# Hybrid DiT trunk step on one core: the norm of branch C's heads in thirds, its factors and the residual gate sent to all partitions through DRAM

## The chip, the cores and the metric

One core of one Trainium2 chip. The metric is the device time of one execution in microseconds (us); smaller is better. The engines are TensorE (PE in the rows; PEld its weight loads), VectorE (DVE), ScalarE (ACT), GpSimd (POOL) and SyncE (SP), which issues every DMA of this kernel.

## The reference

Two layers of a trunk with three branches over 1152 tokens (128 context and 1024 latent), model width 1024. All branches are fed by one projection of the normed stream. What matters here is the end of branch C (differential attention, four heads of width 128) and the end of the layer:

```python
def diff_attn(q, k, v, lam, subln, lam_init):
    ...
        s = jnp.einsum('bqhmd,bshmd->bhmqs', qblk, k).astype(jnp.float32) * SCALE
        p = jax.nn.softmax(s, axis=-1)
        pd = p[:, :, 0] - lam * p[:, :, 1]
        return jnp.einsum('bhqs,bshe->bqhe', pd.astype(v.dtype), v)
    ...
    o = rmsnorm(o, subln) * (1 - lam_init)
    return o.reshape(B, T, D_C)

def mixer_tail(x, gate, oa, g_a, ob, g_b, oc, g_c, merge, P):
    ...
         + m[:, :, 2] * ((oc * jax.nn.silu(g_c)) @ P['w_br_c']))
    return x + gate * (y @ P['w_out'])
```

So each head's output is divided, token by token, by the root of its mean square over 128 channels, scaled per channel, and multiplied by a SiLU gate; and the layer's output is scaled by a gate row per channel (one for context, one for latent tokens) before it is added to `x`.

## The kernel before

The 1152 tokens are 9 tiles of 128. Float32 products are made of three fast products of high and low parts (`mm3`, L162 to L165), so operands are split: a ScalarE copy writes the high part, a VectorE or GpSimd subtraction the low one. A head of branch C is worked off in five groups of at most two tiles. For each group: `q_conv` (L434 to L446) copies the queries twice side by side into `qdup` (one half by VectorE, L437, one by ScalarE), transposes them (L442) and splits them into `qhl`; `c_probs` makes the scores (L540, L541), evacuates them with their row maxima (L542), takes the exponential (L552) and subtracts the two maps; `c_pv` transposes the probabilities (L569), splits them into `PT` and multiplies by V into `ps_o`; its result goes into `u.o`, a tile of 128 channels by 1152 tokens (`O` in the rows).

When a head is complete, `c_finish` (L580) makes its norm. Tokens lie along the free axis there, channels on partitions. ScalarE squares `u.o`; nine matmuls with a column of ones (L585) give the sums with tokens on partitions; a reciprocal root by VectorE (`rsq`, some twenty small operations) gives the 9 columns of factors. To bring a factor per token to all 128 partitions, three times three products of a broadcast column with the identity matrix (L593) write 128 x 384 into PSUM, from which VectorE multiplies (`stt`, L112 in the rows), and GpSimd multiplies with the gate. The head then goes to DRAM (`osp`), from where the tail of the layer reads it.

`gate_rows` (L1035) makes the residual gate for a quarter of the output projection by the same means: 4 products of a broadcast column with the identity (L1040) and two ScalarE copies into `gr`, four quarters a layer. VectorE reads `gr` once for each of the nine token tiles of a quarter.

What sets the order: the program is written as a sequence in Python, and a list scheduler fixes the order of each engine's instructions when the kernel is built; at run time each engine takes its list in order and waits on semaphores. `fg` marks code as foreground (`HPO`, L26, an offset of priority). The projections of the next head, the gates and other work are a generator, `background` (L755), of which `step(n)` (L768) takes n pieces after each group, by the table `BGQ` (L50). `flush` (L736) is called within `fg` after the scores of a group: it runs the pending product with V (`pend`) of the group before, and, one group later, the norm of the finished head (`done`). So a head's norm runs as foreground in the second group of the next head; that of the fourth head runs beside the first groups of branch A.

Tiles come from rings: a tag has a fixed number of buffers (`RINGS`, L54), taken in the order of the program, and a new tile waits until the last use of the one it replaces. Ring `E` has two buffers, and `qdup` lives there; `gr` is in `cx`, with one buffer. PSUM has 4 buffers of tag `s`, 3 of `t` and 1 of `o`.

Of the kernel before, what the change touches and what calls it, by code (L numbers as in the profile page):

```python
# [18 lines left out]
DEPTH = 2  # L19
# [45 lines left out]
def hybrid_dit_kernel(ctx, tc, I, O):  # L65
# [8 lines left out]
    def ps(tag, *shape):  # L74
        return psp.tile([128] + list(shape), F32, tag=tag, name="ps_" + tag, bufs=PSB[tag])

    def tl(tag, *shape, bufs=1):
        return big.tile([128] + list(shape), F32, tag=tag, name=tag, bufs=bufs)

    def al(tag, name, *shape):  # L80

        return big.tile([128] + list(shape), F32, tag=tag, name=name, bufs=RINGS[tag])
# [13 lines left out]
    def dma(out, in_):  # L96
        nc.sync.dma_start(out=out, in_=in_)

    def acopy(out, in_, scale=1.0):
        A.activation(out=out, in_=in_, func=AF.Copy, scale=scale)  # L100

    def tt(e, out, a, b, op):
        e.tensor_tensor(out=out, in0=a, in1=b, op=op)  # L103
# [7 lines left out]
    def stt(out, a, s, b, op0, op1):  # L111
        V.scalar_tensor_tensor(out=out, in0=a, scalar=s, in1=b, op0=op0, op1=op1)  # L112
# [3 lines left out]


    xres = drp.tile([NT, 128, DM], F32, name="xres")
    osp = [drp.tile([4, 128, NTOK], F32, name=f"osp{b}") for b in range(3)]
    xsp, gsp = (drp.tile([4, 128, NTOK], F32, name=n) for n in ("xsp", "gsp"))  # L120

# [456 lines left out]
        acopy(u.o[:, tiles[0] * 128:tiles[0] * 128 + w], po)  # L578

    def c_finish(L, u, h):  # L580
        sq = al("T", "sq", 1152)
        A.activation(out=sq, in_=u.o, func=AF.Square)
        p = ps("t", 9)
        for i in range(9):
            T.matmul(out=p[:, i:i + 1], lhsT=sq[:, i * 128:(i + 1) * 128], rhs=one, start=True, stop=True)  # L585
        e2 = tl("e2", 9)
        stt(e2, u.l0, EPS, u.l0, ALU.mult, ALU.mult)
        y = rsqrt(p, 9, 1.0 / 128, e2)
        for c in range(3):
            pb = ps("t", 3, 128)  # L590
            for t in range(3):
                i = 3 * c + t
                T.matmul(out=pb[:, t, :], lhsT=y[:, i:i + 1].to_broadcast([128, 128]), rhs=ident, start=True, stop=True)  # L593
            oc = u.o[:, c * 384:(c + 1) * 384].rearrange("p (t n) -> p t n", t=3)
            stt(oc, oc, L.D.sub1, pb, ALU.mult, ALU.mult)
            tt(Pq, u.o[:, c * 384:(c + 1) * 384], u.o[:, c * 384:(c + 1) * 384],
               u.gate[:, c * 384:(c + 1) * 384], ALU.mult)
        dma(osp[2][h], u.o)

# [126 lines left out]
    def unit_phase(L):  # L728
# [1 line left out]
        l = L.l  # L730
        a_groups = [CQA, CKA, CVA]
        pend = None

        done = None

        def flush():  # L736
            nonlocal pend, done
            d, done = done, None
            if pend:
                pend()  # L740
                pend = None
            if d:
                d()

        def start(h):
            u = Unit()
# [21 lines left out]
        def step(n):  # L768
            for _ in range(n):
                next(bg, None)  # L770

        def fg(f, *args):
            with tc.high_priority(offset=HPO):
# [258 lines left out]
                tail_branch(L, 2, j, c, ohl, wbs[j], ms[j - 6][:, c, :])  # L1032
                y_split(L, j, c)

    def gate_rows(D, q4, dst):  # L1035

        for s in range(2):
            p = ps("t", 2, 128)
            for k in range(2):
                T.matmul(out=p[:, k, :], lhsT=D.modt[:, 16 + 2 * q4 + k, s:s + 1].to_broadcast([128, 128]),  # L1040
                         rhs=ident, start=True, stop=True)
            acopy(dst[:, s, :], p.rearrange("p k n -> p (k n)"), scale=0.5)

    def x_in(l, i):
        if l:
# [14 lines left out]
    def w_out_phase(L, Ln):  # L1060
        l = L.l
        wtag = ("P", "S", "S", "P")
        wq = [load_wo(L, 0, wtag[0])]
        gr = None
        for q4 in range(4):
            cs = slice(q4 * 256, (q4 + 1) * 256)
            if q4 < 3:
                wq.append(load_wo(L, q4 + 1, wtag[q4 + 1]))
            w = wq[q4]
            gr = al("cx", "gr", 2, 256)  # L1070
            gate_rows(L.D, q4, gr)
            if q4 == 1 and Ln is not None:
                load_unit_consts(Ln)
                Ln.wu = load_wu(Ln, c_groups(0))
# [197 lines left out]
```

## Time and profile before

| | |
|---|---|
| median of 3 runs | 2887.47 us (2887.15 to 2888.11) |
| the profiled execution | 2884.63 us, of which its span is 2882.8 us |
| mean granted clock of TensorE | 0.98 of full speed |
| PE, DVE, ACT, POOL busy | 2740.5, 1773.3, 1284.2, 924.8 us |
| PE share of the span | 95% |

Busy time is that of the instructions themselves; waiting for a semaphore is not in it. In the rows, a line is a line of the kernel before (a helper's line where a helper issues the instruction: L97 is every DMA, L100 ScalarE's copies, L103 a tensor-tensor operation, L107 a tensor-scalar one, L112 `stt`), and buffer numbers are left out of names. "idle before" is how long the engine had stood still just before an instruction, with what released it. The granted clock (`PEclk`) is the share of full speed that TensorE was given in a stretch. The durations below are all from the profiled execution.

### The profile page before, as it was taken

The page shows a single profiled execution, that of the slowest core. Times are in us where ns is not written, and L with a number is a line of the kernel's source. Part 1 is how long each engine was busy: PE and PEld are TensorE (multiplying, and loading weights), DVE is VectorE, ACT ScalarE, POOL GpSimd, SP SyncE. Part 2 cuts the span into 40 slices and gives each one's busy share as a digit, 9 for nine tenths or more (in the row PEclk, how much of TensorE's full clock was granted, in tenths as well). Part 3 has the DMA queues.
Part 4 walks back from the last instruction along what each step waited for, and adds up shares of the span by engine and source line. Part 5 has one row for each costly group of instructions (what it writes and reads, how often), then busy time and mean ns, then how long its engine had stood idle before and what let it go on. Part 6 is the DMA issues. An engine that isn't in the chain of part 4 may idle for free.

```text
span 2882.8 us, 44242 instructions
## 1 busy us (share of the span) xinstructions
PE 2740.5 (95%) x16745; PEld 2648.5 (92%) x16745; DVE 1773.3 (62%) x4412; ACT 1284.2 (45%) x2577; POOL 924.8 (32%) x756
## 2 busy tenths in 40 slices
PE   8999999999998989998999999999999989999999
PEld 4889999999997989998989899998999989899989
DVE  5887878776646583116958887787665455311162
ACT  4464555566654631212144555555666456212110
POOL 1334354531234341213104252445212344322130
PEclk9999999999999999998999999999999999999999
DMA  6011011112222252114631010110112121311122
GB/s 228 25 33 34 19 32 42 36 48 74 70 73 65 65 159 68 52 39 144 195 100 36 22 34 19 33 48 31 55 64 80 63 70 60 114 44 49 49 90 85
DMA packets 231698, 190.74 MB, mean 66 GB/s; under 512 B 21746, under 2 KB 217660, under 8 KB 231484
## 3 DMA queue, kind: packets, MB, share of 16 engines
q1 hardware_dynamic: 231484, 187.92, 20.7%
q8 instruction: 131, 2.15, 0.3%
q14 instruction: 83, 0.68, 0.1%
HBM read 153.52 MB, written 34.35 MB: 65 GB/s over the span
## 4 chain that ended last, share of the span: by engine, by line
PE 71%; DVE 15%; ACT 5%; issue 4%; DMA 3%; POOL 1%; SPq 1%; DVEq 0%; ACTq 0%; POOLq 0%
PE ps_s L163 18%; PE ps_s L164 18%; PE ps_s L165 18%; PE ps_o L711 2%; PE ps_t L702 2%; DVE P L542 2%; PE ps_s L540 2%; DVE macc L112 2%; PE ps_t L569 1%; PE ps_s L541 1%; DMA modw<-in_mod_w_dram 1%; DVE lr L860 1%; DVE lr L112 1%; PE ps_o L164 1%; PE ps_s L662 1%
## 5 line engine op out<-in xcount | busy, mean ns | idle before, releaser
L163 PE MATMUL ps_s<-h,wsh 128*128 128x384 f32 x1920 | 660.0, 344 | 8.6 <-ACT mg L971 5.9
L165 PE MATMUL ps_s<-h,wsl 128*128 128x384 f32 x1920 | 654.4, 341 | 0.9 <-POOL wsl L103 0.9
L164 PE MATMUL ps_s<-h,wsh 128*128 128x384 f32 x1920 | 654.9, 341 | 0.0
L163 PEld LDWEIGHTS ps_s<-h,wsh 128*128 128x128 f32 x1920 | 364.3, 190 | 13.5 <-ACT mg L971 7.1
L165 PEld LDWEIGHTS ps_s<-h,wsl 128*128 128x128 f32 x1920 | 363.1, 189 | 2.0 <-POOL wsl L103 1.6
L164 PEld LDWEIGHTS ps_s<-h,wsh 128*128 128x128 f32 x1920 | 364.1, 190 | 0.6
L103 POOL TENSOR_TENSOR wsl<-wsraw,wsh 128x1024 fp32r<-128x1024 f32 x80 | 198.7, 2483 | 395.3 <-ACT wsh L100 229.6
L163 PE MATMUL ps_s<-uwh,h 128*128 128x384 f32 x864 | 296.9, 346 | 5.8 <-ACT h L100 2.8
L164 PE MATMUL ps_s<-uwl,h 128*128 128x384 f32 x864 | 293.9, 341 | 0.1
L165 PE MATMUL ps_s<-uwh,h 128*128 128x384 f32 x864 | 292.1, 344 | 0.0
L112 DVE SCALAR_TENSOR_TENSOR ps_s<-mg,ps_s 128x384 f32<-128x384 f32 x96 | 52.6, 559 | 359.7 <-PE ps_s L165 359.6
L103 POOL TENSOR_TENSOR qkraw<-qkraw,tab 128x384 f32<-128x384 f32 (+2 forms) x92 | 132.7, 1453 | 335.2 <-DVE qkraw L103 212.5
L542 DVE TENSOR_SCALAR_CACHE_REDUCE P<-ps_s 128x384 f32<-128x384 f32 (+1 forms) x400 | 205.5, 539 | 39.9 <-PE ps_s L541 38.7
L163 PE MATMUL ps_s<-oh,wb 128*128 128x384 f32 x576 | 196.0, 351 | 35.3 <-DVE yr L112 10.5
L103 DVE TENSOR_TENSOR PT<-ps_t,PT 128x512 fp32r<-128x512 f32 (+2 forms) x304 | 187.7, 625 | 59.5 <-ACT PT L100 58.0
L100 ACT ACTIVATE PT<-ps_t 128x512 fp32r<-128x512 f32 (+2 forms) x304 | 160.0, 546 | 125.1 <-PE ps_o L165 67.9
L552 ACT ACTIVATE P<-P,csm 128x1152 f32<-128x1152 f32 (+1 forms) x144 | 165.8, 1154 | 101.8 <-DVE csm L107 101.8
L164 PE MATMUL ps_s<-ol,wb 128*128 128x384 f32 x576 | 194.7, 346 | 0.0
L165 PE MATMUL ps_s<-oh,wb 128*128 128x384 f32 x576 | 194.5, 346 | 0.0
L971 ACT ACTIVATE mg<-ps_s 128x384 f32<-128x384 f32 x144 | 69.6, 485 | 266.1 <-PE ps_s L165 169.6
L163 PE MATMUL ps_s<-woh,yh 128*128 128x256 f32 x576 | 167.4, 291 | 11.7 <-DVE xt L103 6.5
L163 PEld LDWEIGHTS ps_s<-uwh,h 128*128 128x128 f32 x864 | 164.6, 191 | 9.4 <-ACT h L100 3.5
(253 smaller groups left out, 6364.6 us busy)
## 6 DMA issues: line engine op xcount, KB each, us to landing
wsraw<-in_w_in_dram SPq DMA_DIRECT2D x80, 512.0 KB, 3.7
wuraw<-in_w_in_dram SPq DMA_DIRECT2D x72, 192.0 KB, 3.5
ol<-osp SPq DMA_DIRECT2D x24, 576.0 KB, 5.0
modw<-in_mod_w_dram SPq DMA_DIRECT2D x16, 512.0 KB, 5.8
woraw<-in_w_out_dram SPq DMA_DIRECT2D x16, 512.0 KB, 4.4
modw<-in_mod_w_dram SPq DMA_DIRECT2D x14, 576.0 KB, 5.5
modw<-in_mod_w_dram SPq DMA_DIRECT2D x19, 384.0 KB, 4.3
wuraw<-in_w_in_dram SPq DMA_DIRECT2D x36, 128.0 KB, 2.3
```

What stands on the lines that cost most here:

```text
L100: A.activation(out=out, in_=in_, func=AF.Copy, scale=scale)
L103: e.tensor_tensor(out=out, in0=a, in1=b, op=op)
L112: V.scalar_tensor_tensor(out=out, in0=a, scalar=s, in1=b, op0=op0, op1=op1)
L163: T.matmul(out=out, lhsT=r(lh), rhs=r(rh), start=first, stop=False)
L164: T.matmul(out=out, lhsT=r(lh), rhs=r(rl), start=False, stop=False)
L165: T.matmul(out=out, lhsT=r(ll), rhs=r(rh), start=False, stop=last)
L540: T.matmul(out=p, lhsT=qh, rhs=kk, start=True, stop=False)
L542: V.tensor_scalar(out=S[:, n * c:n * c + n], in0=p, scalar1=1.0, scalar2=NEG, op0=ALU.mult, op1=ALU.max, accum_out=mx[:, mp, c:c + 1])
L552: A.activation(out=Ss[mp][:, 0:n], in_=Ss[mp][:, 0:n], func=AF.Exp, scale=0.125, bias=nm[:, mp:mp + 1], accum_out=acc)
L702: T.transpose(p[:, b, 128 * j:128 * j + 128], Ps[2 * t + j][:, (b0 + b) * 128:(b0 + b + 1) * 128], ident)
L711: T.matmul(out=po[:, t, :, :], lhsT=r(vs[kb]), rhs=r(x[:, b, :]), start=kb + k == 0, stop=k == 1 and kb == len(vs) - 1)
L971: A.activation(out=m, in_=p, func=AF.Tanh, scale=0.5)
```

## The change

`c_finish` becomes a generator. The squares are made in thirds of 384 tokens (tiles `sq` in ring E instead of T), the sums of a third are copied to `csum` by VectorE, and after each third it yields. The fourth piece makes the factors, transposes them into 9 rows (one transpose, L597 of the changed kernel), copies them (`yrow`, ring E) and writes the rows to DRAM (`ybd`); then, for each third, a DMA reads the three rows back to all 128 partitions (`yb`, ring E), VectorE multiplies from there, and GpSimd as before. `flush` no longer runs the norm but makes the generator `fin`, and `step` takes one piece of it beside each piece of `bg`; what remains is run when the next head's norm begins. `gate_rows` transposes the 16 columns of the gate once per layer (two transposes), and writes 8 rows to DRAM (`gbd`); for each quarter two DMAs read the rows of `gr` to all partitions.

```diff
+    ybd = drp.tile([4 * DEPTH, NT, 128], F32, name="ybd")
+    gbd = drp.tile([DEPTH, 8, 2, 128], F32, name="gbd")
...
     def c_finish(L, u, h):
-        sq = al("T", "sq", 1152)
-        A.activation(out=sq, in_=u.o, func=AF.Square)
-        p = ps("t", 9)
-        for i in range(9):
-            T.matmul(out=p[:, i:i + 1], lhsT=sq[:, i * 128:(i + 1) * 128], rhs=one, start=True, stop=True)
+
+        sums = tl("csum", 9)
+        for c in range(3):
+            sq = al("E", "sq", 384)
+            A.activation(out=sq, in_=u.o[:, c * 384:(c + 1) * 384], func=AF.Square)
+            p = ps("t", 3)
+            for t in range(3):
+                T.matmul(out=p[:, t:t + 1], lhsT=sq[:, t * 128:(t + 1) * 128], rhs=one, start=True, stop=True)
+            V.tensor_copy(sums[:, 3 * c:3 * c + 3], p)
+            yield
         e2 = tl("e2", 9)
         stt(e2, u.l0, EPS, u.l0, ALU.mult, ALU.mult)
-        y = rsqrt(p, 9, 1.0 / 128, e2)
+        y = rsqrt(sums, 9, 1.0 / 128, e2)
+        p = ps("t", 128)
+        T.transpose(p[0:9, :], y, ident)
+        row = al("E", "yrow", 128)
+        acopy(row[0:9, :], p[0:9, :])
+        yd = ybd[4 * L.l + h]
+        dma(yd, row[0:9, :])
         for c in range(3):
-            pb = ps("t", 3, 128)
-            for t in range(3):
-                i = 3 * c + t
-                T.matmul(out=pb[:, t, :], lhsT=y[:, i:i + 1].to_broadcast([128, 128]), rhs=ident, start=True, stop=True)
-            oc = u.o[:, c * 384:(c + 1) * 384].rearrange("p (t n) -> p t n", t=3)
-            stt(oc, oc, L.D.sub1, pb, ALU.mult, ALU.mult)
-            tt(Pq, u.o[:, c * 384:(c + 1) * 384], u.o[:, c * 384:(c + 1) * 384],
-               u.gate[:, c * 384:(c + 1) * 384], ALU.mult)
+            oc = u.o[:, c * 384:(c + 1) * 384]
+            yb = al("E", "yb", 3, 128)
+            dma(yb, yd[None, 3 * c:3 * c + 3, :].to_broadcast([128, 3, 128]))
+            stt(oc, oc, L.D.sub1, yb.rearrange("p t n -> p (t n)"), ALU.mult, ALU.mult)
+            tt(Pq, oc, oc, u.gate[:, c * 384:(c + 1) * 384], ALU.mult)
         dma(osp[2][h], u.o)
+        yield
...
             if d:
-                d()
+                for _ in fin:
+                    pass
+                fin = d() or iter(())
...
         def step(n):
             for _ in range(n):
                 next(bg, None)
+                next(fin, None)
...
-    def gate_rows(D, q4, dst):
-
+    def gate_rows(D):
+
+        p = ps("t", 2, 128)
         for s in range(2):
-            p = ps("t", 2, 128)
-            for k in range(2):
-                T.matmul(out=p[:, k, :], lhsT=D.modt[:, 16 + 2 * q4 + k, s:s + 1].to_broadcast([128, 128]),
-                         rhs=ident, start=True, stop=True)
-            acopy(dst[:, s, :], p.rearrange("p k n -> p (k n)"), scale=0.5)
+            T.transpose(p[0:8, s, :], D.modt[:, 16:24, s], ident)
+        row = al("E", "grow", 2, 128)
+        acopy(row[0:8], p[0:8], scale=0.5)
+        dma(gbd[D.l], row[0:8])
...
-        gr = None
+        gate_rows(L.D)
         for q4 in range(4):
...
             gr = al("cx", "gr", 2, 256)
-            gate_rows(L.D, q4, gr)
+            for s in range(2):
+                dma(gr[:, s, :].rearrange("p (k n) -> p k n", k=2),
+                    gbd[l, 2 * q4:2 * q4 + 2, s, :][None].to_broadcast([128, 2, 128]))
```

Lines of the changed kernel are two higher up to `c_finish`: its L444 is L442 of before, its L571 is L569, its L542 is L540, its L439 is L437. The order of the instructions changes at three places around the norm of a head; all three are shown for the first head of layer 0, whose norm runs in the second head. In the names, `ps_s<-uwh,h` and `ps_s<-uwl,h` are matmuls of the projection of the next head, `qdup` and `qhl` a group's queries before and after the transposes, `P` and `PT` probabilities, `O` the finished head.

First place: TensorE, at the identity products and at the next query transposes behind them. Before, the products,

```order
L163 MATMUL ps_s_2453<-uwh_2032,h_290 128x384
L593 MATMUL ps_t_2374<-ident_63,rsq_2360 128x128 x3
L593 MATMUL ps_t_2380<-ident_63,rsq_2360 128x128 x3
L593 MATMUL ps_t_2386<-ident_63,rsq_2360 128x128 x3
L164 MATMUL ps_s_2453<-uwl_2033,h_290 128x384
L165 MATMUL ps_s_2453<-uwh_2032,h_291 128x384
```

then seven more matmuls of the projection, and then:

```order
L164 MATMUL ps_s_2453<-uwl_2041,h_296 128x384
L165 MATMUL ps_s_2453<-uwh_2040,h_297 128x384
L442 MATMUL ps_t_2517<-ident_63,qdup_2513 128x128 x4
L569 MATMUL ps_t_2559<-ident_63,P_2302 128x128
L569 MATMUL ps_t_2559<-ident_63,P_2394 128x128
L569 MATMUL ps_t_2559<-ident_63,P_2302 128x128
```

Now, at the transpose of the factors:

```order
L165 MATMUL ps_s_2722<-uwh_2042,h_298 128x384
L597 MATMUL ps_t_2704<-ident_63,rsq_2690 9x128
L166 MATMUL ps_s_2722<-uwl_2043,h_298 128x384
L167 MATMUL ps_s_2722<-uwh_2042,h_299 128x384
L444 MATMUL ps_t_2786<-ident_63,qdup_2782 128x128
L571 MATMUL ps_t_2828<-ident_63,P_2495 128x128
L571 MATMUL ps_t_2828<-ident_63,P_2596 128x128
L571 MATMUL ps_t_2828<-ident_63,P_2495 128x128
L444 MATMUL ps_t_2786<-ident_63,qdup_2782 128x128
L571 MATMUL ps_t_2828<-ident_63,P_2596 128x128
L444 MATMUL ps_t_2786<-ident_63,qdup_2782 128x128 x2
L571 MATMUL ps_t_2842<-ident_63,P_2495 128x128
```

The products are gone; one transpose stands in a run of the projection's matmuls, whose last two stand between it and the query transposes.

Second place: VectorE, at the products with the factors. Before:

```order
L112 SCALAR_TENSOR_TENSOR P_2394<-P_2407,csm_2393,P_2394 128x1152
L112 SCALAR_TENSOR_TENSOR O_1350<-O_1350,sub1_529,ps_t_2374 128x384
L112 SCALAR_TENSOR_TENSOR O_1350<-O_1350,sub1_529,ps_t_2380 128x384
L112 SCALAR_TENSOR_TENSOR O_1350<-O_1350,sub1_529,ps_t_2386 128x384
L437 COPY qdup_2980<-uq_952 128x4x64
L103 TENSOR_TENSOR qhl_2516<-ps_t_2517,qhl_2516 128x512
L393 TENSOR_REDUCE qkss_2481<-qktmp_2480 128x12
L542 TENSOR_SCALAR P_2525,csm_2524<-ps_s_2526 128x384
```

Now:

```order
L112 SCALAR_TENSOR_TENSOR O_1352<-O_1352,sub1_531,yb_2709 128x384
L103 TENSOR_TENSOR rsq_2756<-rsq_2756 128x12
L112 SCALAR_TENSOR_TENSOR O_1352<-O_1352,sub1_531,yb_2713 128x384
L103 TENSOR_TENSOR rsq_2756<-rsq_2756 128x12
L439 COPY qdup_2782<-uq_954 128x4x64
L112 SCALAR_TENSOR_TENSOR rsq_2756<-rsq_2756 128x12
```

and, five small operations of `rsqrt` later:

```order
L112 SCALAR_TENSOR_TENSOR O_1352<-O_1352,sub1_531,yb_2717 128x384
L112 SCALAR_TENSOR_TENSOR rsq_2756<-rsq_2756 128x12
L439 COPY qdup_2991<-uq_954 128x4x64
L103 TENSOR_TENSOR qkraw_2748<-qkraw_2748,rsq_2756 128x768
L103 TENSOR_TENSOR PT_2833<-ps_t_2828,PT_2833 128x512
L103 TENSOR_TENSOR qhl_2785<-ps_t_2786,qhl_2785 128x512
```

The three products, which stood together, are spread between operations of another `rsqrt` (`rsq_2756`, of the projection's queries and keys); the `qdup` that L444 above reads now stands behind the second of them, and the next `qdup` behind the third.

Third place: ScalarE, in the changed kernel from the copy of the factors on. Its copy for `qdup_2782` and that for `qdup_2991` take the ring's buffers after `yb_2713` and `yb_2717`:

```order
L100 ACTIVATE yrow_2706<-ps_t_2704 9x128
L100 ACTIVATE uvr_2048<-ps_s_2722 128x128
L100 ACTIVATE qkraw_2748<-ps_s_2722 128x256
L394 ACTIVATE qktmp_2749<-qkraw_2748 128x768
L100 ACTIVATE uwh_3205<-wuraw_3201 128x1152
L100 ACTIVATE qdup_2782<-uq_954 128x4x64
L100 ACTIVATE uwh_3213<-wuraw_3209 128x1152
L100 ACTIVATE PT_2833<-ps_t_2828 128x512
L100 ACTIVATE qdup_2991<-uq_954 128x4x64
L100 ACTIVATE qhl_2785<-ps_t_2786 128x512
```

Before, no tile of the norm stood in that ring, and ScalarE had no copy of the factors.

## Rows read from the trace of the kernel before

**Rows 1.** The page: busy time of each engine (part 1), and the chain (part 4).

```profile
PE 2740.5 (95%) x16745; PEld 2648.5 (92%) x16745; DVE 1773.3 (62%) x4412; ACT 1284.2 (45%) x2577; POOL 924.8 (32%) x756
...
PE 71%; DVE 15%; ACT 5%; issue 4%; DMA 3%; POOL 1%; SPq 1%; DVEq 0%; ACTq 0%; POOLq 0%
```

**Rows 2.** Windows: branch C's heads, layers 0 and 1 (columns in the first row).

```profile
core 0: us, PE busy (x) PEld busy (x) DVE busy (x) ACT busy (x) POOL busy (x), PEclk, DMA share, GB/s
217.00:545.00 328.00, 317.21 (x2030) 307.06 (x2029) 261.41 (x832) 170.65 (x352) 140.52 (x151) 0.98 0.10 30
1700.00:1980.00 280.00, 269.84 (x1734) 262.06 (x1733) 222.56 (x700) 147.63 (x306) 123.90 (x128) 0.99 0.11 34
```

**Rows 3.** Timeline of PE around one head's identity products (start us, us, what).

```profile
238.61 0.34 PE L163 MATMUL ps_s<-uwh,h 128*128 128x384 f32 x1
238.78 2.17 PE L593 MATMUL ps_t<-ident,rsq 128*128 128x128 f32 x18
240.71 0.42 PE L164 MATMUL ps_s<-uwl,h 128*128 128x384 f32 x1
```

**Rows 4.** Waits of PE (line <- releaser: us in total, times, longest).

```profile
PE ps_s L540 <- DVE P L542: 7.7, 14, 1.4
...
PE ps_t L593 <- DVE rsq L112: 2.9, 2, 1.5
```

**Rows 5.** Lines L593, L1040 on PE: ns min/median/max, first and last start.

```profile
L593 PE MATMUL ps_t<-ident,rsq x144: 273/275/376, 238.8 to 1971.8; 128*128 128x128 f32 x144
...
L1040 PE MATMUL ps_t<-ident,modt x64: 270/275/356, 1142.1 to 2853.1; 128*128 128x128 f32 x64
```

**Rows 6.** Windows: behind a norm's sums, first and last of five dips (columns: rows 2).

```profile
227.00:230.50 3.50, 2.13 (x9) 1.07 (x8) 3.50 (x13) 0.89 (x1) 3.09 (x5) 1.00 0.07 21
230.50:234.00 3.50, 3.48 (x12) 3.28 (x11) 3.50 (x18) 1.70 (x4) 0.00 (x0) 0.53 0.00 0
1865.70:1869.20 3.50, 3.50 (x13) 3.50 (x12) 3.50 (x18) 0.00 (x0) 3.42 (x6) 0.52 0.07 21
```

**Rows 7.** Groups of ACT in branch C of layer 0 (busy us, mean ns of one).

```profile
L100 ACT ACTIVATE uvr<-ps_s 128x128 f32<-128x128 f32 x24 | 6.6, 273 | 39.4 <-PE ps_s L165 39.3
```

**Rows 8.** DMA issues: count, KB each, median us to landing.

```profile
wuraw<-in_w_in_dram SPq DMA_DIRECT2D x72, 192.0 KB, 3.5
...
xsp<-xt SPq DMA_DIRECT2D x24, 192.0 KB, 1.8
...
out_dram<-uvr SPq DMA_DIRECT2D x10, 64.0 KB, 1.6
out_dram<-ukr SPq DMA_DIRECT2D x10, 64.0 KB, 2.2
...
lt<-in_lam_k_dram SPq DMA_DIRECT2D x4, 32.0 KB, 5.9
```

**Rows 9.** Tile wuraw: SyncE's issue (ns), and all loads to landing.

```profile
L97 SPq DMA_DIRECT2D wuraw<-in_w_in_dram x108: 367/471/2272, 13.0 to 1921.2; - x108
...
DMA to landing us min/median/max: 2.2/2.7/9.7
```

**Rows 10.** Groups of DVE in branch C of layer 0 (busy us, mean ns of one).

```profile
L103 DVE TENSOR_TENSOR PT<-ps_t,PT 128x512 fp32r<-128x512 f32 x48 | 32.7, 686 | 6.7 <-ACT PT L100 6.4
...
L103 DVE TENSOR_TENSOR rsq<-rsq 128x12 f32<-128x12 f32 x66 | 11.1, 168 | 1.3
L103 DVE TENSOR_TENSOR qkraw<-qkraw,rsq 128x768 f32<-128x768 f32 x11 | 10.5, 957 | 0.2
...
L112 DVE SCALAR_TENSOR_TENSOR O<-O,sub,ps_t 128x384 f32<-128x384 f32 x12 | 7.4, 614 | 2.5 <-PE ps_t L593 2.1
...
L437 DVE COPY qdup<-uq 128x256 f32<-128x256 f32 x14 | 6.4, 457 | 12.0 <-issue 4.7 <-PE ps_t L442 4.5 <-POOL uv L103 2.4
```

**Rows 11.** Timeline of PE at a group's query transposes and first scores.

```profile
252.33 0.60 PE L442 MATMUL ps_t<-ident,qdup 128*128 128x128 f32 x4
252.68 0.42 PE L540 MATMUL ps_s<-ck,qhl 128*128 128x384 f32 x1
```

**Rows 12.** Windows: two gaps of PE and what follows (columns as in rows 2).

```profile
871.00:876.80 5.80, 0.04 (x1) 0.00 (x0) 5.80 (x11) 0.52 (x1) 0.70 (x1) 0.91 0.34 108
876.80:883.00 6.20, 6.19 (x20) 6.20 (x21) 1.49 (x4) 1.83 (x4) 4.64 (x5) 0.53 0.21 57
923.00:930.00 7.00, 2.60 (x15) 2.06 (x13) 7.00 (x11) 0.77 (x2) 2.34 (x1) 1.00 0.22 78
930.00:934.00 4.00, 4.00 (x14) 3.68 (x15) 0.46 (x1) 1.95 (x4) 3.98 (x4) 0.57 0.28 78
```

**Rows 13.** Timeline of DVE in the output projection of layer 1.

```profile
2835.43 0.42 DVE L103 TENSOR_TENSOR xt<-ps_s,gr 128x256 f32<-128x256 f32 x1 [1.97 <-PE ps_s L165]
...
2838.28 0.43 DVE L103 TENSOR_TENSOR xt<-ps_s,gr 128x256 f32<-128x256 f32 x1 [1.97 <-DMA out_dram<-xt]
```

More of the change, by code (lines that the diff above doesn't have):

```diff
@@ L734, in unit_phase @@
         done = None
+        fin = iter(())
         def flush():
-            nonlocal pend, done
+            nonlocal pend, done, fin
             d, done = done, None
```

## The prediction

> **What bounds the kernel now.** I began with the page. TensorE is busy for 95% of the span and holds 71% of the chain that ended last, against 15% for VectorE [rows 1]. So a microsecond in which TensorE stands still is paid in full, and one of TensorE's work that goes away is gained in full, unless another wait takes its place. Then I took the two stretches in which branch C's heads run, one per layer. There the windows show TensorE busy for 317.2 of 328 us and 269.8 of 280 us, with VectorE second at 261 and 223 us [rows 2]. These stretches are nearly full, with 21 us idle in both together; a new wait here has no idle time to hide in. The third view is what surrounds the norm of a head. The 18 instructions of L593 (9 identity products, two passes each) run from 238.78 to 240.71 us between two matmuls of the same projection, with no gap on either side [rows 3]: 1.93 us, 0.107 us each. The reader should see that the old norm costs TensorE its own time and next to no waiting. TensorE's list of waits gives L593 only 2.9 us in the whole run [rows 4].
>
> **What goes away.** The products: 8 heads times 1.93 us is 15.4 us [rows 3], less eight transposes, four of which take 0.35 us at L442 [rows 11], 0.09 each: 14.7 us. Their waits: 2.9 us [rows 4]. The residual gate's products: 64 instructions [rows 5] at 0.107 us make 6.8 us, less four new transposes, 0.4 us: 6.4 us. Together about 24 us, all of it TensorE's own time. The 144 instructions of the sums stay, in threes. Behind five of the eight norms' sums there is also a clock dip: in the first TensorE is busy for 2.13 of 3.5 us and then runs at a granted clock of 0.53, the lower of its two levels (1.2 of 2.4 GHz), for 3.5 us; the last has 0.52 [rows 6]. That is about 1 us of wait, of a kind that the list has as "L540 <- P L542", 7.7 us in 14 waits [rows 4], and 3.5 times 0.47, 1.6 us, of clock: 13 us for five. Thirds may spread what leads to it; 0 to 13 us, of which I take 6.
>
> **What is added: a trip to DRAM that TensorE waits for.** The order on TensorE (first place) shows the factors' transpose, L597 of the changed kernel, only two projection matmuls ahead of the next group's query transposes (its L444, the L442 of before), and those need `qdup`. The order on VectorE (second place) has `qdup` after the products of thirds 0 and 1, which wait for `yb`; and the three tiles share the ring E of two buffers, so `qdup` can't be written before the second `yb` has been used. The queue behind that is TensorE's whole list: it is in order, and only the two matmuls (2 x 0.17 us, [rows 3]) stand between. Before, L442 stood 11 projection matmuls behind the products, and its `qdup` wasn't among the rows behind the norm's products on VectorE at all. All eight heads have this form (in each layer's last head not even the two matmuls).
>
> The time from the end of L597, step by step. The nearest row to the transpose is L593, 0.27 us [rows 5]. The copy to `yrow` is ScalarE's 128x128 copy from PSUM, 0.27 us [rows 7]. The write of 4.6 KB: the stores of 64 KB land in 1.6 and 2.2 us, those of 192 KB in 1.8 [rows 8]; I take 1.8. The read of 192 KB to all partitions has the shape of `wuraw` (128 x 3 x 128, 512 B runs), which lands in 3.5 us; below lies the fastest `wuraw`, 2.2 us [rows 9], above the slowest of the small broadcasts, 5.9 us [rows 8] (a single `wuraw` of 9.7 us I leave out). I take 3.5 since bytes and packets are the same. So the first `yb` lands at 0.27 + 0.27 + 1.8 + 3.5 = 5.8 us; the second is issued right behind (0.4 us, [rows 9]) and is covered by the first product. VectorE then does product, a piece of rsqrt, product, another piece and `qdup`: 0.61 + 0.17 + 0.61 + 0.17 + 0.46 = 2.0 us [rows 10]. `qdup` is there at 7.9 us, and TensorE, out of work at 0.35, has **stood still for 7.5 us**.
>
> The second wait comes from the third `yb`. It takes the buffer of the first, so it is issued at 5.8 + 0.6 = 6.4 us and lands at 9.9. Its product stands on VectorE ahead of `qkraw`, `PT` and `qhl` (second place): 0.61 + 0.17 + 0.46 + 0.96 + 0.69 us [rows 10] puts the low half of `PT` at 12.8 us. ScalarE has the same trouble: its half of the next `qdup` waits for that buffer ahead of `qhl` (third place). From 7.9 us on TensorE has 12 transposes at 0.09 us [rows 11], one product with V (0.1) and four scores of 0.17: 1.9 us in all. It **stands still for another 12.8 - 7.9 - 1.9 = 3.0 us**. That is 10.5 us a head and 84 us for eight. With the short ends (1.6 and 2.2 us) the same sum is 6.0 + 1.8 = 7.8 us a head, 62 us; with the long ones (2.2 and 5.9) 10.3 + 5.5 = 15.8 us, 126 us.
>
> The Trainium skill, "DMA: Bandwidth & Descriptors", section "Anatomy of one DMA — SWDGE (gpsimd) path", gives a transfer some 2.0 us fixed, whatever its size, and bytes over 436e3 on top; it is for another issuing path, and speaks against sending 4.6 KB through DRAM at all. By it, as an estimate, the write would be 2.0 and the read 2.45 us, and the sum 8.6 us a head, 69 us, some 15 us less than by the rows. The 64 KB stores at 1.6 us [rows 8] are below its fixed part, and the 3.5 us loads above its line.
>
> After a stall the clock falls: after TensorE's gap of 5.8 us at 871 us it was granted 0.53 for the next 6.2 us, after 4.4 us of standing still before 930 it had 0.57 for 4 us [rows 12]; 0.47 x 6.2 = 2.9 us lost, 0.43 x 4 = 1.7. Here most of the low stretch falls into the second stall, where a slow TensorE costs little; I take 1 us a head, 8 us, between 0 and 23.
>
> **Edits costed at nothing.** The squares in thirds are ScalarE's, which is 52% busy here [rows 2]; the copies to `csum` are 24 on VectorE of the size of rsqrt's pieces, 0.17 us [rows 10], and VectorE is 80% busy at most [rows 2]; the osp stores come later but are read only in the tail. The gate rows now wait for a load at each quarter of the output projection: `gr` has one buffer, so the load starts after the last use by VectorE. VectorE uses it every 2.85 us there and idles 1.97 us of that [rows 13]; four PSUM tiles cover about 11 us against a load of 2.3 to 5.9 us [rows 8]. If that cover were gone, it would cost 6 switches times up to 5.9 us, 35 us.
>
> **The sum.** -24 - 6 + 84 + 8 = +62 us on the profiled execution's 2884.6 makes 2947 us. The median of the runs shown is 2.8 us (0.1%) above the profiled execution, which is small beside the range; I leave the number at 2947.
>
> **The rivals.**
> (1) *Faster*: the stall does not come about. Its place is L444; it decides by whether `qdup` is written before TensorE reaches it. The break-even is 30 us over eight heads, 3.7 us a head. With no stall only the savings count: 2884.6 - 30 = about 2855 us. For it: the trip is short beside a head of some 76 us (608 us for eight, [rows 2]). Against it: the order is fixed when the kernel is built, and the write and one read alone are 3.8 us at their fastest [rows 8, 9] against 0.35 us of cover; so what would have to be wrong is the reading of the order. 0.07.
> (2) *Only the first wait*: `yb` 2 comes early or the low halves are not needed so soon. 8 x 7.5 = 60, and 60 + 8 - 30 = +38, 2923 us; with the short ends, no clock and all of the 13 us, 48 - 37 = +11, 2896 us. For it: ScalarE and VectorE idle elsewhere in the head; against it, the order of both. 0.25.
> (3) *The clock stays low*: two stalls close together, each followed by a low stretch as in [rows 12]. 23 instead of 8 us: 2962 us, and with loads a microsecond slower than I take (one in each of the two waits, 2 us a head) 2978. 0.10.
> (4) *The gate rows' loads come late too*: +35 on top, 2982 us, if the load queues behind other loads on SyncE for over 11 us; against it, the slack of [rows 13]. 0.03.
> That the "background" does nothing is no case of its own: the first two thirds' sums do stand ahead among earlier scores, the rest does not.
>
> **How the numbers follow.** The forecast, both waits, has 0.50; by its bounds it reaches from 62 - 37 = +25, 2910 us, to 126 - 24 + 23 = +125, 3010 us; the upper end needs every load at the slowest row, and I stop at 2988, which is every load and write at its long end with the clock as I take it, or loads near 5.2 us with the worst of the clock. With (2) to (4) the range is 2896 to 2988, with some 0.15 outside, (1) among it. This kernel's measurement can tell about 0.2%, 5.8 us, from no change. Faster 0.07 is (1); same 0.05 is a trip near break-even; slower 0.88 is the rest.
>
> **What would show it.** Right: TensorE's waits list L444 for VectorE's or ScalarE's `qdup`, eight times, 6 to 8 us each, and a second wait at the products with V or the scores, some 3 us; VectorE waits for `yb`, and `yb` lands 5 to 6 us after L597; the clock drops behind it. L593 and L1040 are gone. Wrong: if L444 shows no wait, the mechanism falls and the time is below that of before; if the waits are there but shorter than 4 us, the DMA prices are wrong; if the output projection shows waits for `gr`, it was (4).

## The result, and the profile after

The changed kernel took 2992.82 us (median of 4 runs, 2991.46 to 2994.08) against 2887.79 us for the kernel before: a ratio of 1.0361, 95% interval [1.0343, 1.0379]. It is 105 us slower; forecast were 2947 us and a range of 2896 to 2988. The direction was right, the size was not: the loss against before is 105 us where 59 were forecast.

| profiled execution | before | after |
|---|---|---|
| span | 2882.8 us | 2992.3 us |
| PE busy | 2740.5 us | 2746.6 us |
| span less PE busy | 142.3 us | 245.7 us |
| DVE busy | 1773.3 us (4412 instructions) | 1863.8 us (4436) |
| mean granted clock | 0.98 | 0.958 |

The lines of the page after that answer to [rows 1]:

```profile
PE 2746.6 (92%) x16549; PEld 2648.8 (89%) x16549; DVE 1863.8 (62%) x4436; ACT 1292.1 (43%) x2587; POOL 917.4 (31%) x756
...
PE 66%; DVE 19%; DMA 5%; ACT 5%; issue 4%; POOL 2%; SPq 1%; DVEq 0%; ACTq 0%; POOLq 0%
```

TensorE stands still for 103 us more; its busy time rises by 6 us although some 22 us of its work went away, so nearly 30 us went to the lower clock. VectorE is busy for 90 us more with 24 more instructions. The list of TensorE's waits in the changed kernel (line <- releaser: us in total, times, longest) answers to [rows 4]:

```profile
PE ps_t L444 <- DVE qdup L439: 62.2, 8, 8.1
PE ps_t L597 <- DVE rsq L112: 25.1, 8, 7.5
...
PE ps_s L542 <- ACT qhl L100: 17.0, 7, 2.7
```

The three make 104 us, all of the new standstill. Two were forecast: L444, 7.8 us a head (7.5 in the prediction), and the scores behind it, 2.1 us a head (3.0). The wait at L597 for the factors was not: 25 us, of which six heads have 1.6 to 1.7 us each and the last head of each layer 7.5. The timeline of TensorE at the norm of the first head shows all three, with the idle time before an instruction in brackets:

```profile
267.09 0.28 PE L597 MATMUL ps_t<-ident,rsq 128*9 128x128 f32 x1 [1.67 <-DVE rsq L112]
...
267.39 0.34 PE L167 MATMUL ps_s<-uwh,h 128*128 128x384 f32 x1
275.59 0.45 PE L444 MATMUL ps_t<-ident,qdup 128*128 128x128 f32 x1 [7.86 <-DVE qdup L439]
...
281.19 1.65 PE L542 MATMUL ps_s<-ck,qhl 128*128 128x384 f32 x4 [2.60 <-ACT qhl L100]
```

And the windows around it (columns as in [rows 2]):

```profile
263.00:270.00 7.00, 3.06 (x17) 2.41 (x15) 6.20 (x7) 3.46 (x6) 3.81 (x3) 1.00 0.30 86
270.00:281.00 11.00, 3.00 (x13) 2.74 (x13) 10.76 (x20) 3.25 (x6) 8.46 (x5) 0.50 0.47 126
281.00:288.00 7.00, 6.80 (x30) 6.20 (x30) 5.28 (x13) 1.22 (x3) 5.95 (x10) 0.56 0.35 122
```

From 270 to 287 us the granted clock is 0.50, the lower level, so of the 9.8 us that TensorE is busy between 270 and 288 nearly half is lost. Such a low stretch of some 17 us stands behind each norm; before, five norms had one of some 3.5 us [rows 6].

Matched instruction by instruction, the two traces lie 5 us apart when the heads of layer 0 begin, 37 us after three of its heads and 57 us after the fourth; in layer 1 the difference goes from 56 over 91 to 109 us. From the end of the heads to the end of the layer it changes by less than 3 us.

### The profile page after: what moved, and what is told of

It reads as the page before. It is cut to its first block, busy times and chain, and to the rows that moved or that the text cites. A ratio compares the mean times of both kernels' runs of the same rounds, so it can differ in the third digit from the quotient of the medians.

```text
span 2992.3 us, 44038 instructions
## 1 busy us (share of the span) xinstructions
PE 2746.6 (92%) x16549; PEld 2648.8 (89%) x16549; DVE 1863.8 (62%) x4436; ACT 1292.1 (43%) x2587; POOL 917.4 (31%) x756
## 4 chain that ended last, share of the span: by engine, by line
PE 66%; DVE 19%; DMA 5%; ACT 5%; issue 4%; POOL 2%; SPq 1%; DVEq 0%; ACTq 0%; POOLq 0%
PE ps_s L165 16%; PE ps_s L166 16%; PE ps_s L167 16%; DVE rsq L103 2%; DVE macc L112 2%; PE ps_s L542 2%; PE ps_o L722 2%; DVE P L544 2%; PE ps_t L571 2%; PE ps_s L543 2%; PE ps_t L713 2%; DVE lr L874 1%; DMA out_dram<-xt 1%; DMA modw<-in_mod_w_dram 1%; DVE lr L112 1%
## 5 line engine op out<-in xcount | busy, mean ns | idle before, releaser
L103 POOL TENSOR_TENSOR qkraw<-qkraw,tab 128x384 f32<-128x384 f32 (+2 forms) x92 | 126.2, 1382 | 346.4 <-DVE qkraw L103 272.1
L103 POOL TENSOR_TENSOR uwl<-wuraw,uwh 128x1152 fp32r<-128x1152 f32 (+1 forms) x36 | 89.7, 2493 | 307.5 <-ACT uwh L100 297.6
```

## The experiments

Each kernel was timed in three rounds against the kernel before on the same chip (before: 2887.3 to 2889.1 us in the three sets). Differences are against before's time of the same set, or against after's 2993 us, which was taken in a set of its own (before: 2887.8 there); between sets they are good to 1 or 2 us.

**1. The norm in the background, without DRAM.** `c_finish` keeps its thirds and yields; the factors go by identity products, as in the removed lines of the diff, and the residual gate is that of before.

> The norm in thirds in the background as in the changed kernel, but the factors by identity products into PSUM as before, and the residual gate as before: no trip to DRAM, no yb in ring E. Theory (the standstill is the DRAM trip, which qdup in ring E waits for): the waits at L444 (62 us) and at the scores behind it (17 us) go, with some 20 us of clock; the wait for rsqrt at the products (25 us in the changed kernel) stays; about 2900 us, between 2885 and 2915. Rival (the norm in the background makes the factors so late that TensorE stands still however they are spread): the waits only move to the products, and the time stays above 2950 us.

Measured: 2910.3 us, 1.0070 [1.0055, 1.0085] of before. TensorE's waits:

```profile
PE ps_t L598 <- DVE rsq L112: 16.6, 8, 4.1
```

As the theory had it: L598, the products, waits for the factors as L597 did, and the long waits are gone. The background placement, with the thirds and without DRAM, costs 21 us.

**2. No loads.**

```diff
-            yb = al("E", "yb", 3, 128)
-            dma(yb, yd[None, 3 * c:3 * c + 3, :].to_broadcast([128, 3, 128]))
-            stt(oc, oc, L.D.sub1, yb.rearrange("p t n -> p (t n)"), ALU.mult, ALU.mult)
+            stt(oc, oc, L.D.sub1, L.cos.rearrange("p i n -> p (i n)")[:, 0:384], ALU.mult, ALU.mult)
```

The product reads a table in place of `yb`, so the heads are not normed.

> The changed kernel without the loads of yb: VectorE multiplies by a table that is always in SBUF (the factors are made, transposed and written to DRAM, but not used). Theory: qdup needs no yb, so the wait at L444 falls from 7.8 us a head to under 1 us and that at the scores goes; the wait for rsqrt at L597 stays near 25 us; about 2900 us, 2890 to 2915. Rival (late factors and a VectorE held up by GpSimd): L444 or L597 go on waiting for more than 60 us together, above 2950 us.

Measured: 2934.6 us, 1.0151 [1.0134, 1.0168]; 58 us less than after. That is outside what either had said:

```profile
PE ps_t L597 <- DVE rsq L112: 41.4, 8, 9.4
...
PE ps_t L444 <- ACT qdup L100: 4.0, 6, 0.7
```

The trip is gone from L444, but the wait for the factors grew from 25 to 41 us. So the theory was right on the trip and had sized a second cause too low, for which it kept 25 us: the factors are late.

**3. Loads that nothing reads.** `yb` is loaded into ring E as in the change; the product reads the table of experiment 2.

> The changed kernel with the loads of yb into ring E, but VectorE multiplies by a table that is always in SBUF: nobody but the ring waits for the loads, and the products don't wait for DRAM. Theory (it is the ring): qdup still waits for its buffer until the load has landed, 0.3 + 0.3 + 1.3 + 3.9 us after L597, so L444 waits 5 to 7 us a head; 2955 to 2985 us. Rival (it is the products that stand ahead of qdup on VectorE and wait for yb): L444 waits under 3 us a head, 2900 to 2930 us.

Measured: 2962.8 us, 1.0252 [1.0234, 1.0270].

```profile
PE ps_t L444 <- ACT qdup L100: 38.2, 6, 6.4
PE ps_t L597 <- DVE rsq L112: 31.2, 8, 4.4
...
PE ps_t L444 <- DVE qdup L439: 13.8, 2, 6.9
```

52 us in 8 waits at L444, 6.5 us a head, with nobody reading `yb`: as the theory had it, the ring alone makes TensorE wait for the trip. The other 30 us between this run and after come with the products' reading of `yb`.

**4. The residual gate alone.** The kernel before with the new `gate_rows`.

> The kernel before with the change of the residual gate alone. Theory (the loads of gr come late, six waits of VectorE of 27 us in the changed kernel, of which TensorE sees 5 us, and the clock falls behind two of them): what L1040 gave back, 6.4 us, goes there again; within 0.3% of before, 2884 to 2895 us. Rival (the loads are hidden, as predicted): 6 us faster, 2881 us.

Measured: 2889.7 us, 1.0001 [0.9991, 1.0010]. The saving of L1040 does not arrive. What waits in the output projections, by the tile `gr` (us, times):

```profile
  DMA gr<-gbd: 27.6, 4
...
  PE ps_s L164: 6.0, 3
```

VectorE waits 27.6 us in four places for the loads, TensorE 6.0 us for VectorE behind them.

**5. A short factor chain.** The reciprocal root is cut to its first operation, so the factors are not the norm's:

```diff
-        y = rsqrt(sums, 9, 1.0 / 128, e2)
+        y = tl("ysh", 9)
+        stt(y, sums, 1.0 / 128, e2, ALU.mult, ALU.add)
```

> The changed kernel with the reciprocal root of the norm cut to its first operation (one VectorE operation in place of thirteen; the factors are not the norm's). Theory (two waits that add up: the late factors at L597, 25 us, and the DRAM trip at L444 and the scores, 79 us): L597 waits under 5 us, L444 stays at 7 to 8 us a head; 2960 to 2975 us. Rival (the trip alone sets the end, L597's wait is only part of the same wait and moves to L444): 2985 us or more.

Measured: 2941.5 us, 1.0186 [1.0169, 1.0203]; 51 us less than after, below the theory's range and twice what the wait at L597 holds.

```profile
PE ps_t L444 <- DVE qdup L439: 48.1, 8, 7.8
...
PE ps_s L542 <- ACT qhl L100: 1.2, 1, 1.2
```

L597 has no wait left, L444 fell to 6.0 us a head, and the second wait at the scores went from 17 us to 1.2. But the edit also changed the order: with the short chain the scheduler put the transpose of the factors 20 projection matmuls ahead of L444 in six heads, where after has two, so some 3 us more of the trip are covered there (L444 starts 9.1 to 9.3 us behind the transpose, in after 8.5). The 51 us are what a short chain is worth together with the order that it brings; how they divide was not measured.

**6. The same trip, as foreground.**

```diff
-                for _ in fin:
-                    pass
-                fin = d() or iter(())
+                for _ in d() or ():
+                    pass
```

> The changed kernel, with the norm run whole and as foreground, where it was before, not in steps beside the background: the trip to DRAM stays. Its order has L597 eight to nine projection matmuls ahead of L444 in heads 0 to 2. Theory (the background placement costs the wait for rsqrt, the trip costs the rest): L597 waits under 8 us, L444 6 to 7 us a head (1.5 us of cover); 2945 to 2970 us. Rival (the placement is what costs, the trip is then covered): under 2915 us.

Measured: 2941.3 us, 1.0184 [1.0167, 1.0201]; 51 us less than after, and a little under the theory's range. L597 has no wait, L444 still has 53 us:

```profile
PE ps_t L444 <- DVE qdup L439: 42.4, 7, 7.2
...
PE ps_t L444 <- ACT qdup L100: 10.6, 3, 5.9
```

So the placement is worth as much as the length of the chain, and the trip costs whatever the placement. With experiments 1 and 12, all with the sums in thirds, this is a square: foreground and products 2884, background and products 2910, foreground and DRAM 2941, background and DRAM 2993 us. (The two with DRAM also have the new gate rows, which experiment 4 finds to be worth nothing.) The trip costs 58 us in the foreground and 83 in the background.

**7. Factors early, a step for each load and product.** The sums and `rsqrt` are those of before and run in `flush`; then

```diff
+        yield
+        p = ps("t", 128)
...
+        dma(yd, row[0:9, :])
+        for c in range(3):
+            yield
+            yb = al("E", "yb", 3, 128)
+            dma(yb, yd[None, 3 * c:3 * c + 3, :].to_broadcast([128, 3, 128]))
+            yield
+            oc = u.o[:, c * 384:(c + 1) * 384]
```

> Sums and rsqrt whole and as foreground as before (gate rows as before too); the transpose, the write and each load and each product a background step of its own, a load one step ahead of its use. In the order qdup waits for the write at most, not for a yb. Theory (the trip costs because qdup waits for it in ring E and TensorE for qdup): L444 under 1.5 us a head, L597 under 1 us a head; what is saved is the 15 us of products: 2873 to 2895 us. Rival (VectorE's in-order wait for yb holds up the evacuation of scores whatever the ring): above 2905 us.

Measured: 2920.4 us, 1.0115 [1.0093, 1.0137], the rival's side. L443 (the query transposes) has 9.3 us in all, L593 (the factors' transpose) 4.7: the ring's part of the theory holds. But

```profile
  DMA yb<-ybd: 25.5, 13
```

VectorE stands still for 25.5 us in 13 places for `yb`, in order, with evacuations behind it. TensorE stands still for 30 us more than before (172.7 against 142.3), some 20 of them in these places or within 3 us behind them. A trip that is taken out of the ring still blocks a queue.

**8. More buffers for `gr`.** Experiment 4 with `gr` in ring W, which has seven.

> The gate rows through DRAM as in e4_gate_only, but gr in ring W (seven buffers, free at that time), so a quarter's load need not wait for the last use of the one before. Theory (one buffer is why the loads come late): no wait of VectorE for gr, and the 6.4 us of L1040 are kept: 2879 to 2886 us. Rival (the products with the identity cost nothing there, the projection waits for VectorE or weights anyway): 2887 to 2892 us.

Measured: 2894.8 us, 1.0024 [1.0015, 1.0033]; neither. VectorE's wait for `gr` fell to 6.1 us in one place, nearly as the theory had it, but in layer 0 another wait of TensorE came up, for the sums of the next layer's modulation,

```profile
PE ps_t L315 <- DVE macc L112: 16.6, 6, 7.7
```

which was 5.4 us in experiment 4. How the ring leads to it was not followed up; what the trace shows is that GpSimd now waits once for a `gr` to be read, 40.3 us, before it writes the `uwl` that shares the ring.

**9 and 10. What holds the chain.** The low halves of the head weights by VectorE, once in the changed kernel, once in the kernel before:

```diff
-            split(hi, lo, raw, "A", "P")
+            split(hi, lo, raw, "A", "V")
```

> The changed kernel with the low halves of the head weights (uwl, 36 subtractions of 2.5 us) made by VectorE in place of GpSimd. Theory (a VectorE operation on two SBUF operands stands still while a GpSimd operation runs: 91 of the 702 operations of rsqrt end when a GpSimd operation ends, 99 us too long in all, 47 of it behind uwl; before 23 operations and 26 us): the operations of rsqrt that last over 1 us fall by half or more, L597 waits under 15 us in place of 25, and in spite of some 43 us more VectorE work the time falls, 2950 to 2980 us. Rival (the chain is slow since VectorE has too much to do): more VectorE work makes it worse, 2995 us or more.

> The control for e9: the kernel before with the same move of uwl to VectorE. Theory: only 20 us of rsqrt's operations were behind uwl before and TensorE didn't wait for them, so nothing is gained and the added VectorE work costs 0 to 20 us: 2885 to 2910 us. Rival (the move helps by itself, whatever the norm): below 2875 us.

Measured: 2954.4 us, 1.0230 [1.0215, 1.0246], 38 us less than after; and 2884.2 us, 0.9989 [0.9979, 0.9998], 3 us less than before. Of the 702 operations of `rsqrt`, those that last over 0.27 us, 0.1 more than usual: 91 in after, 99 us too long in all; 63 and 45 us in experiment 9; 25 and 26 us before (23 in the expectation); 14 and 4 us in experiment 10. All 91 end within 0.1 us of the end of a GpSimd operation. The second wait is gone, with the loads in place and the transpose two matmuls ahead of L444 as in after; L597 waits 18.6 us, over the 15 that the theory gave:

```profile
PE ps_t L597 <- DVE rsq L112: 18.6, 8, 4.2
...
PE ps_s L542 <- ACT qhl L100: 2.3, 2, 1.2
```

In six heads L597 still waits 1.7 us, since the nine-column operations of the norm's own chain stand behind other GpSimd work and are as long as in after; in the last head of each layer it waits 4.2 in place of 7.5.

```profile
L103 DVE TENSOR_TENSOR rsq<-rsq 128x12 f32<-128x12 f32 x228 | 45.1, 198 | 5.0
...
L103 DVE TENSOR_TENSOR rsq<-rsq 128x9 f32<-128x9 f32 x48 | 37.2, 775 | 1.0
```

What follows: VectorE got 36 more subtractions and the kernel 38 us faster, against 3 us in the control (some 8 of the 38 lie ahead of the first head, where the control gains 5). It is GpSimd that lengthens the chain, not the amount of VectorE's work. The control shows it in another way too: VectorE's busy time stays at 1773 us although it makes 36 subtractions of 1.2 us more, so some 43 us of it had been such waits before as well, and TensorE had not waited for them.

**11. Neither loads nor chain.** Experiments 2 and 5 together.

> Both of e2 and e5: the changed kernel without the loads of yb and with the reciprocal root cut to one operation (products by a table; the factors are not the norm's). Theory (late factors and the DRAM trip are all of it): the standstills at L597, L444 and the scores go, TensorE idles 140 to 155 us in the run as before, and what is left is the saved products against the gate rows: 2875 to 2900 us. Rival (something else in the background placement or the gate rows costs too): above 2910 us.

Measured: 2875.4 us, 0.9958 [0.9944, 0.9973]. The line of the page:

```profile
PE 2730.1 (95%) x16549; PEld 2625.1 (91%) x16549; DVE 1777.6 (62%) x4340; ACT 1286.8 (45%) x2587; POOL 940.4 (33%) x756
```

Its span is 2873.6 us, so TensorE's standstill is 143.5 us, that of before (142.3), and neither L444 nor L597 has a wait for the norm. TensorE is busy for 10 us less than before, 12 short of the work saved; the rest is spread over many lines, 1 or 2 us each. 51 us for the late chain (with its order, experiment 5) and 58 for the loads make 109 of the 117 us between this and after. Nothing else of size is left.

**12. Only the sums in thirds.** The kernel before with the sums in thirds (the added lines of the diff up to `csum`), all run in one go at the old place; products and gate rows as before.

> A version that might beat both: the kernel before with the sums alone in thirds (squares in ring E, three sums at a time, as in the change), all of it foreground at its old place, products with the identity and gate rows as before. Theory (the nine sums in a row and the wait around them bring the clock down behind five norms, 13 us in all; in thirds they stand between other matmuls): fewer dips, 2876 to 2886 us. Rival (the squares now take ring E's buffers from qdup, and wait): 2890 us or more.

Measured: 2883.6 us, 0.9986 [0.9977, 0.9996]. The windows at the first three norms show the clock at full speed, where [rows 6] shows a dip:

```profile
225.00:240.00 15.00, 14.62 (x90) 13.35 (x89) 13.57 (x53) 6.19 (x12) 6.93 (x12) 1.00 0.02 5
325.00:340.00 15.00, 14.24 (x88) 12.89 (x87) 13.58 (x54) 6.61 (x13) 6.47 (x12) 1.00 0.02 5
425.00:440.00 15.00, 13.96 (x81) 12.49 (x80) 12.95 (x54) 6.82 (x14) 7.43 (x13) 1.00 0.02 5
```

This is the part of the change that is worth keeping: 4 us less than before. Experiment 10's 3 us could be added; both together were not run.

## Why the prediction was right or wrong

**The place and the first mechanism: right.** Order and ring put TensorE behind the trip at L444, eight times: 62.2 us against 60 forecast. Experiment 3 shows the ring, experiment 2 the loads. The trip itself was priced well. The timeline of SyncE at the first head (start us, us) shows the write at 267.70 and the reads that wait for it at 268.99:

```profile
267.70 0.30 SPq L97 DMA_DIRECT2D ybd<-yrow  x1
268.99 0.83 SPq L97 DMA_DIRECT2D yb<-ybd  x2
...
273.77 0.34 SPq L97 DMA_DIRECT2D yb<-ybd  x1
```

1.3 us from the write's issue to the next issue, where I took 1.8; and by the trace's records of completed transfers the 24 loads landed 2.9 to 4.1 us after their issue, where I took 3.5. Counted from the start of L597, the second `yb` was there after 6.2 to 6.5 us at most heads (6.2 in the prediction), and `qdup` after 8.4 (7.9).

**The savings: right.** Counted from one start to the next on TensorE, without standstills, the identity products' 15.8 us became 1.0 us of transposes, and the gate's 7.0 us became 0.5: 21 us of work, as forecast, beside the 2.9 us of waits. The five dips went, but other and longer ones took their place.

**The step that failed: the chain of factors.** I took the waits at the products (2.9 us, [rows 4]) as gone and priced VectorE's operations by their means, 0.17 us for a piece of `rsqrt` [rows 10]. The changed order puts these pieces (thirteen to a `rsqrt`, not some twenty) where GpSimd is busy. VectorE's timeline at the first head (start us, us):

```profile
263.58 3.25 DVE L103 TENSOR_TENSOR rsq<-rsq 128x9 f32<-128x9 f32 x2
...
270.48 2.61 DVE L107 TENSOR_SCALAR rsq<-rsq 128x12 int32<-128x12 int32 x2
...
273.13 0.61 DVE L112 SCALAR_TENSOR_TENSOR O<-O,sub,yb 128x384 f32<-128x384 f32 x1
...
276.78 2.48 DVE L112 SCALAR_TENSOR_TENSOR rsq<-rsq 128x12 f32<-128x12 f32 x1
...
279.59 0.61 DVE L112 SCALAR_TENSOR_TENSOR O<-O,sub,yb 128x384 f32<-128x384 f32 x1
```

and GpSimd's:

```profile
264.46 2.35 POOL L103 TENSOR_TENSOR wsl<-wsraw,wsh 128x1024 fp32r<-128x1024 f32 x1
...
270.38 2.61 POOL L103 TENSOR_TENSOR uwl<-wuraw,uwh 128x1152 fp32r<-128x1152 f32 x1 [3.57 <-ACT uwh L100]
...
276.58 2.65 POOL L103 TENSOR_TENSOR uwl<-wuraw,uwh 128x1152 fp32r<-128x1152 f32 x1 [0.27 <-ACT uwh L100]
```

Three times a row of one or two small operations lasts until GpSimd's operation ends: 263.58 + 3.25 = 266.83 beside 264.46 + 2.35 = 266.81; 273.09 beside 272.99; 279.26 beside 279.23. The first delays L597. The second delays the products little: by the records of completed transfers the first `yb` landed at 272.75 and was used at 273.13; `qdup` is then late by some 0.8 us more through an operation held at 274.27. The third delays the product with the third `yb`, which had landed at 276.70, by 2.3 us, and with it the scores.

In the last head of each layer the chain is late in another way. Its operations have their usual length there, but they stand in VectorE's list behind the reduction `qkss` of the projection, for which VectorE waits for ScalarE, and ScalarE for GpSimd (the timeline at the norm of layer 0's fourth head):

```profile
573.29 0.16 DVE L591 COPY csum<-ps_t 128x3 f32<-128x3 f32 x1
...
585.93 0.84 ACT L394 ACTIVATE qktmp<-qkraw 128x768 f32<-128x768 f32 x1 [4.00 <-POOL aq L103]
...
586.81 0.95 DVE L395 TENSOR_REDUCE qkss<-qktmp 128x12 f32<-128x768 f32 x1 [4.75 <-ACT qktmp L394]
...
590.46 0.38 PE L597 MATMUL ps_t<-ident,rsq 128*9 128x128 f32 x1 [7.55 <-DVE rsq L112]
```

The last third's sums were there at 573.45, the chain began at 587.88, and L597 waited 7.5 us; with the same in layer 1 this is 15 of its 25 us. The forecast had no term for either kind of lateness.

Groups of VectorE over the whole run, after:

```profile
L103 DVE TENSOR_TENSOR rsq<-rsq 128x12 f32<-128x12 f32 x228 | 57.2, 251 | 5.3
...
L103 DVE TENSOR_TENSOR rsq<-rsq 128x9 f32<-128x9 f32 x48 | 37.1, 774 | 1.0
...
L112 DVE SCALAR_TENSOR_TENSOR O<-O,sub,yb 128x384 f32<-128x384 f32 x24 | 17.7, 740 | 9.9 <-DMA yb<-ybd 9.8
```

and before:

```profile
L103 DVE TENSOR_TENSOR rsq<-rsq 128x12 f32<-128x12 f32 x228 | 40.8, 179 | 5.1
...
L103 DVE TENSOR_TENSOR rsq<-rsq 128x9 f32<-128x9 f32 x48 | 9.5, 197 | 0.5
```

The norm's own chain (128x9) takes four times as long in the background, 774 against 197 ns; in the foreground of experiment 12 the same group has 168 ns. VectorE's waits for `yb` are few in after (9.8 us in 4 places, all in the layers' last heads): elsewhere, while the loads were under way, VectorE mostly stood inside such an operation, which the profile counts as busy. Taking away the long chain frees 51 us (part of it by the order), the loads 58, and both together 117.

The Trainium skill, "SBUF — State Buffer", section "SBUF: two separate sides", says that VectorE and GpSimd share one pair of ports, and that a VectorE operation with two SBUF inputs, or in what it calls a 2-port perf mode, and a GpSimd operation that reads SBUF shut each other out for the whole instruction. The trace agrees: all 91 operations of `rsqrt` that last too long end within 0.1 us of GpSimd's. Of the three above, those at 263.58 and 276.78 have two SBUF inputs; the one at 270.48 has one, as have 25 of the 91, and no run here tells whether these are in such a mode. It also fits that three of the 24 products, which read PSUM before (614 ns, [rows 10]) and now read `yb` in SBUF, last 1.5 to 1.8 us and end 0.4 us after a GpSimd operation; the others still take 614.

**The clock: sized too low.** I took 8 us, between 0 and 23; some 30 us were lost. The 30 us are what TensorE's busy time lost at the lower level, 79 us against 49 before, so the five dips that went are counted in. I had taken the low stretch to be 6.2 us [rows 12]; it is 17 us here, as the stalls at L597, L444 and the scores follow one another, and reaches into the work behind the second wait. With the one stall of experiment 2, 3.8 us at most heads, it is 6.8 us; with the two of experiment 3 mostly 10.2.

**The gate rows: costed at nothing, cost what they saved.** Four PSUM buffers did not cover the load; in experiment 4 VectorE waits 27.6 us and TensorE 6.0 us. Rival (4) had the place right; its price of 35 us was far too high.

**The second wait: about right in after, for another reason.** 17.0 us against 24. The third load had landed 2.9 us before its product began, and experiment 9 removes the wait (2.3 us left) with the loads in place, so it was the held operation at 276.78 us rather than the third load that set it. That the size came near was luck.

By terms: forecast -24 - 6 + 84 + 8 = +62; measured, in the profiled executions: -25 for the work and its waits, +79 for the two waits, +25 for L597, some +30 for the clock, in sum +109 as the spans have it (109.5). Some 5 us of it lie ahead of the first head, where the order is the same: the granted clock of the first 222 us is 0.96 in place of 0.98, which is about as much. Why it was lower is not explained; other runs of this study had 1 to 4 us there.

## What to carry to other kernels

Before a small product on TensorE is replaced by a trip through DRAM, see in the order what stands right behind the result: a tile ring with few buffers and an in-order queue turn 5 to 6 us of latency into more than that of standstill at each use, and 1.9 us of products were cheaper by far. When a chain of small VectorE operations is moved into the background, look at what stands ahead of it in VectorE's list, and at what GpSimd does there: an operation that lasts ten times its usual time and ends with a GpSimd instruction is a wait that the profile shows as busy. And take a bundle apart: here the thirds of the sums were worth 4 us, and everything that came with them cost 110.

## What the runs showed of the hardware that was not expected

VectorE's operations of 0.17 us lasted up to 3.25 us for two, beside GpSimd subtractions of 2.4 to 2.7 us, and VectorE's busy time grew by 90 us with 24 more instructions. After three stalls close together TensorE's clock stayed at 0.50 for 17 us, also while it was busy again; after one stall of 5.8 us it had been 6.2 us [rows 12]. Moving 36 subtractions of 2.5 us from GpSimd to VectorE, where they take 1.2 us, made VectorE's busy time smaller (1840.6 us against 1863.8).
